# Weights of an output projection split during the attention heads, in buffers shared with a gated unit

## The chip, the cores and the metric

The kernel runs on one core of a Trainium2 chip. The metric is the device time of one launch in microseconds (us), lower is better. The kernel before takes 1459.13 us, the median of three runs (1458.34 to 1462.85).

TensorE multiplies matrices into PSUM banks (in the profile PE, and PEld for its weight loads), VectorE is DVE, ScalarE is ACT, GpSimd is POOL, and SyncE (SP) issues nearly all transfers. Each engine works through its own instructions in the order in which the program's scheduler has put them.

## The reference

One layer of a decoder, for 1024 prompt tokens and 8 x 4 sample tokens, all in float32:

```python
z  = h @ w_in                                # q, k, v, forget logits, SSM input u
a  = attention(q, k, v, log f)               # 8 heads x 64, causal, decay bias
s  = S5(u);  s = gelu(s);  s = s * sigmoid(s @ w_glu + b_glu)
h1 = LN1(alpha * h + concat(a, s) @ w_out)   # w_out: 1024 x 1024
e  = sigmoid(h1 @ w_pg + b_pg) * (p @ w_pe)
h2 = LN2(alpha * h1 + relu(h1 @ w_up)**2 @ w_down + e)
```

The sample tokens attend to a paged cache of 512 rows each (`cache_k`, `cache_v`).

## The kernel before, in words

Products are exact to nearly float32: each operand is split into a rounded high part and the remainder (`split`, line 156: a cast on ScalarE, then a subtraction, mostly on VectorE), and three matmuls are summed.

The stages follow each other: the input norm and the value projection, the SSM with the other projections (to 300 us), the heads (313 to 521 us), the output projection with LN1 (to 650 us), the embedding gate, and the feed-forward block (from 740 us).

**The gated unit** (`glu`, line 1069) runs in the background of the first heads, with tiles of its own pool `glu`: four `yf`, two `sg`, one `mo` (lines 1055 to 1060). `fill` (line 921) takes a step of a background generator wherever it is called: first all of `glu`, then `sample` (line 931), the attention of the sample tokens. That one loads 64 cache pages (`pg`, 256 KB each) through six buffers and works on through the tail of the last head.

**A head** has two halves. `weights(h)` (line 859) makes the scores of one block of 128 queries: two matmuls to a bank, a minimum on VectorE with the mask `msk`, the exponential on ScalarE into `row`. `values(h)` (line 887) goes through 12 blocks: transposes of `row`, a copy `pe` on ScalarE, a cast `ph` on VectorE, the remainder `pl` on POOL, two matmuls with the values into `po`. At the end of each half of the tokens the result `oh` goes to DRAM (line 916). The scores run one head ahead of the values. The operands of a head (`qa`, `qb`, `ka`, `kb`) come in eight loads (`loads`, line 840) into a pool `attq`, two buffers each, two heads ahead.

**The tail of the last head** starts when its scores are done. The pool `attq` closes (line 1151). In its room and behind it come `h1p`, for the normed stream (line 1152), and `woa`, for the split blocks 4 to 7 of `w_out` (line 1154), which belong to the SSM half of the projection. `load_wo` (line 1157) loads a block of 512 KB into one of two shared buffers `raw` and splits it; lines 1164 to 1165 do so for blocks 4 to 7. `half(i, 4)` (line 1176) then loads the SSM half of token tile i (`mx`, in the same `raw` buffers, line 1171), splits it, and multiplies it by these blocks; this is interleaved with the last eight steps of head 7's values (line 1229). The reciprocals of the softmax sums (`rl`, transposed into `rlt`) go out to DRAM and come back as `rb`. Then the attention pool closes (line 1233), blocks 0 to 3 are loaded and split in its room (line 1236), and the loop at line 1282 does the rest of the projection, tile by tile.

**What sets the order.** The program is traced in the order of the code; a scheduler then orders each engine's instructions by its own simulated times, earlier-traced ones first among those that are ready. So a load may be issued long before its place in the code: in the trace of before, two of the `w_out` blocks are loaded at 282.7 and 320.4 us, but split at 493 us. `tc.issue_after(x)` keeps what is traced under it behind the instruction x, and `newest` (line 165) is the last one traced on an engine.

Of the kernel before, what the change touches and what calls it, by code (L numbers as in the profile page):

```python
# [8 lines left out]
F32 = mybir.dt.float32  # L9
# [9 lines left out]
D = 1024  # L19
# [50 lines left out]
def fox_s5_step(tc, a, o):  # L70
# [85 lines left out]
    def split(x, hi, lo, e=V):  # L156
        S.copy(hi, x)  # L157
        tt(e, lo, x, f(hi), SUB)
# [665 lines left out]

    psum("psB", s=3, t=2, o=1, f=2)
    ptag[0] = "f"
    qctx, actx, h1bctx, h1ctx, smctx, gctx = (ExitStack() for _ in range(6))
    h1x = pool("h1x", stack=h1ctx, side="right")
    aq_ = pool("attq", 2, stack=qctx, side="right")
    gp = pool("glu", stack=gctx, side="right")  # L830

    def slot(j, d=F32R):
        return (h1x, h1b)[j // 2].tile([128, 2 * L * CB], d, tag=f"u{j}", name="u", bufs=1)

    msk = aq_.tile([128, 512], F32, name="msk", bufs=1)
    G.memset(msk[:, 0:384], 0.0)
    G.tensor_copy(msk[:, 384:512], cst[:, TRI:TRI + 128])
    ins_, vs_, rows = {}, {}, {}

    def loads(h):  # L840
        hs_ = slice(h * 64, h * 64 + 64)
        qa = aq_.tile([128, T], F32R, tag="qa", name="qa")
        qb = aq_.tile([68, T], F32R, tag="qb", name="qb")
        ka = aq_.tile([128, T], F32R, tag="ka", name="ka")
        kb = aq_.tile([68, T], F32R, tag="kb", name="kb")
        for j in range(2):
            SY.dma_start(out=f(qa[j * 64:j * 64 + 64]), in_=qd[0, hs_, 0:T])
            SY.dma_start(out=f(ka[j * 64:j * 64 + 64]), in_=kkd[j, hs_, 0:T])
        SY.dma_start(out=f(qb[0:64]), in_=qd[1, hs_, 0:T])
        SY.dma_start(out=f(kb[0:64]), in_=kkd[0, hs_, 0:T])  # L850
        SY.dma_start(out=f(qb[64:68]), in_=cad[h, 0:4])
        SY.dma_start(out=f(kb[64:68]), in_=cad[h, 4:8])
        ins_[h] = qa, qb, ka, kb
# [33 lines left out]
    def values(h):  # L887
        hs_ = slice(h * 64, h * 64 + 64)
        vr = vs_.pop(h)
        vv = ap_.tile([128, 8, 2, HD], F32R, tag="vv", name="vv")  # L890
        V.tensor_copy(vv[:, :, 0], vr)
        tt(G, vv[:, :, 1], vr, f(vv[:, :, 0]), SUB)
        for u in range(2):
            po = bank("po", "o")
            for j in range(4 * u + 4):
                i0 = max(j, 4 * u)
                n = 512 * (u + 1) - 128 * i0
                t = bank("tw", "t")[:, 0:n]
                for i in range(i0, 4 * u + 4):
                    PE.transpose(t[:, (i - i0) * 128:(i - i0) * 128 + 128], rows[h, i][:, j * 128:j * 128 + 128], ident)  # L900
                ph = ap_.tile([128, 512], F32R, tag="ph", name="ph", bufs=3)[:, 0:n]
                pl = ap_.tile([128, 512], F32R, tag="pl", name="pl", bufs=3)[:, 0:n]
                pe = ap_.tile([128, 512], F32, tag="pe", name="pe", bufs=4)[:, 0:n]
                S.copy(pe, t)
                V.tensor_copy(ph, pe)  # L905
                tt(G, pl, pe, f(ph), SUB)
                o = po[:, 512 - n:512]
                v = vv[:, j].rearrange("p a d -> p (a d)")
                PE.matmul(o, lhsT=v, rhs=ph, start=(j == 0), stop=False, skip_group_check=True)
                PE.matmul(o, lhsT=v, rhs=pl, start=False, stop=(j == 4 * u + 3), skip_group_check=True)  # L910
                yield
            ol = ap_.tile([64, 512], F32, tag="ol", name="ol", bufs=1)
            S.copy(ol, po[64:128])
            oh = ap_.tile([64, 512], F32, tag="oh", name="oh", bufs=2)
            tt(V, oh, po[0:64], ol, ADD)
            SY.dma_start(out=mixd[hs_, u * 512:u * 512 + 512], in_=oh)

# [134 lines left out]
    NB = L * CB  # L1052
    ys = []

    for n in range(2):
        gp.tile([128, NB], F32, tag="sg", name="sg", bufs=2)
    gp.tile([128, NT], F32, tag="mo", name="mo")

    def load_y(m):
        t = gp.tile([128, NB], F32, tag="yf", name="yf", bufs=4)  # L1060
        if m < 3:
            SY.dma_start(out=t, in_=yd[m])
        else:
# [5 lines left out]
    def glu():  # L1069
# [15 lines left out]
            yield 0.0  # L1085
        for m in range(4):
            hi, lo = (x[:, :, m % 2 * 128:m % 2 * 128 + 128] for x in w[m // 2])
            sg = gp.tile([128, NB], F32, tag="sg", name="sg", bufs=2)
            yf = ys[m]
            cuts = ((0, 364), (364, 364), (728, 360))  # L1090
            pgs = [bank("mmg", t) for t in "ffo"] if m == 0 else [None] * 3
# [11 lines left out]
                S.activation(out=sg[:, c0:c0 + n], in_=ps[:, :n], func=AF.Tanh, scale=0.5, bias=bglu[:, m:m + 1])  # L1103
                yield 1.85 if m else 0.0
            ts(V, sg, sg, 0.5, MUL, 0.5, ADD)
            mo = gp.tile([128, NT], F32, tag="mo", name="mo")
            yv = yf.rearrange("p (l c) -> p c l", l=L)
            sv = sg.rearrange("p (l c) -> p c l", l=L)
            tt(V, mo[:, 0:T].rearrange("p (c l) -> p c l", l=L), yv[:, 0:NC], sv[:, 0:NC], MUL)
            tt(V, mo[:, T:NT].rearrange("p (b t) -> p b t", t=4), yv[:, NC:CB, 4:8], sv[:, NC:CB, 4:8], MUL)  # L1110
            SY.dma_start(out=mixd[AW + 128 * m:AW + 128 * m + 128], in_=mo)
        gctx.close()

    ahead = (x for h in range(H) for x in weights(h))

# [8 lines left out]
    h1b = pool("h1b", stack=h1bctx)  # L1124
    bp = pool("smp", 2, stack=smctx)
    ap_ = pool("att", 2, stack=actx)
    bg += [glu(), sample(bp)]
    lsum = ap_.tile([128, H, 12], F32, name="lsum", bufs=1)
    fill(1e-3)
    vload(0)  # L1130
    for i in range(4):
        steps(1)
        fill(5)
        if i == 1:
            loads(1)
    for h in range(H - 1):
        for j, _ in enumerate(values(h)):
            if j < 4 or j % 2:
                steps(1)
# [8 lines left out]
        steps(1)  # L1148
        fill(.3)
    steps(1)  # L1150
    qctx.close()
    h1p = pool("h1", stack=h1ctx, side="right")
    woctx = ExitStack()
    woa = pool("woa", stack=woctx, side="right")
    wo = {}

    def load_wo(k, p, q, e=V):
        hi, lo = (p.tile([128, D], F32R, name=f"wo{n}{k}") for n in "hl")
        raw = q.tile([128, D], F32, tag="raw" if q is wp else "z", name="rawo", bufs=2 if q is wp else 3)
        SY.dma_start(out=raw, in_=a["w_out"][0][k * 128:(k + 1) * 128])  # L1160
        split(raw, hi, lo, e)
        wo[k] = hi, lo

    for k in range(4, 8):
        load_wo(k, woa, wp, V)
    mixv = mixd.rearrange("(k p) t -> p k t", p=128)
    dv = "p (c n) -> p c n"
    mxs, pss, order = {}, {}, [0, 1, 2, 3, 4, 5, 8, 6, 7]

    def load_mx(i):  # L1170
        mx = wp.tile([128, KD, 128], F32, tag="raw", name="mx", bufs=2)
        t0, r = tiles[i]
        SY.dma_start(out=mx[:, 4:8, :r], in_=mixv[:, 4:8, t0:t0 + r])
        return mx, [wp.tile([128, KD, 128], F32R, tag=t, name=t, bufs=2) for t in ("whi", "wlo")]

    def half(i, k0):
        t0, r = tiles[i]
        if k0:
            mxs[i] = load_mx(i)
            pss[i] = [bank("pso", t) for t in ("ss", "so")[order.index(i) % 2]]  # L1180
        mx, (mh_, ml_) = mxs[i]
        ks_ = slice(k0, k0 + 4)
# [32 lines left out]
            rb = rbs.pop(i)  # L1215
            tt(V, mx[:, 0:4, :r], mx[:, 0:4, :r], rb[:, :, :r], MUL)

    rl = ap_.tile([128, H, 8], F32, name="rl", bufs=1)
    tt(V, lsum[:, :, 4:8], lsum[:, :, 4:8], lsum[:, :, 8:12], ADD)
    V.reciprocal(rl, lsum[:, :, 0:8])  # L1220
    t = bank("trl", "t")[0:64, 0:128]
    PE.transpose(t, rl.rearrange("p h i -> p (h i)"), ident)
    rlt = ap_.tile([64, 128], F32, name="rlt", bufs=1)
    S.copy(rlt, t)
    SY.dma_start(out=rld.rearrange("h (i c) -> (h i) c", c=128), in_=rlt)
    for i in range(2):
# [7 lines left out]
    op = pool("out", 2, stack=smctx)  # L1234
    wop = pool("wob", stack=woctx, side="right")
    for k in range(4):
        load_wo(k, wop, op, V)
        next(ssm, None)
        fill(.5)
    for _ in ssm:  # L1240
# [2 lines left out]
        load_at(i)  # L1243


    ub = {(kh, 0): [h1p.tile([128, 4, HN], F32R, name=f"u{n}{kh}") for n in "hl"] for kh in range(2)}
    pend = []

    def gate(w, th, tag):
# [518 lines left out]
```

## Time and profile before

| | us |
|---|---|
| median of three runs | 1459.13 |
| the profiled execution | 1462.21 |
| its span, first to last instruction | 1460.4 |
| TensorE busy | 1383.8 |
| VectorE busy | 977.6 |
| POOL busy | 675.6 |
| ScalarE busy | 634.9 |
| mean granted clock of TensorE | 0.977 of 2.4 GHz |

The table shows one profiled execution; its time stands 3.1 us above the median. Busy times are unions of an engine's instructions. A row of the windows view gives a stretch, its length, the busy time and number of instructions of PE, PEld, DVE, ACT and POOL in it, TensorE's granted clock (1.00 is 2.4 GHz, 0.50 is 1.2 GHz), the share of the 16 DMA engines' time that was used, and GB/s. A timeline row gives an instruction's start and duration, and in brackets how long its engine was idle before it and what ended that.

### The profile page before, as it was taken

The page shows a single profiled execution, that of the slowest core. Times are in us where ns is not written, and L with a number is a line of the kernel's source. Part 1 is how long each engine was busy: PE and PEld are TensorE (multiplying, and loading weights), DVE is VectorE, ACT ScalarE, POOL GpSimd, SP SyncE. Part 2 cuts the span into 40 slices and gives each one's busy share as a digit, 9 for nine tenths or more (in the row PEclk, how much of TensorE's full clock was granted, in tenths as well). Part 3 has the DMA queues.
Part 4 walks back from the last instruction along what each step waited for, and adds up shares of the span by engine and source line. Part 5 has one row for each costly group of instructions (what it writes and reads, how often), then busy time and mean ns, then how long its engine had stood idle before and what let it go on. Part 6 is the DMA issues. An engine that isn't in the chain of part 4 may idle for free. (4 is left out here: it accounts for less than half of the span.)

```text
span 1460.4 us, 26638 instructions
## 1 busy us (share of the span) xinstructions
PE 1383.8 (95%) x10045; PEld 1268.7 (87%) x10045; DVE 977.6 (67%) x1579; ACT 634.9 (43%) x1188; POOL 675.6 (46%) x639
## 2 busy tenths in 40 slices
PE   6997999979999889999999999999999999999796
PEld 4887898967766656789999999999999999999786
DVE  7559599648877735657846555545455888788567
ACT  4333434445775623543325444444456443434212
POOL 4313012025665500018846433443347787777845
PEclk7999999989999989999999999999999999999998
DMA  7574355596776564313233444344457345546922
GB/s 275 177 136 105 89 153 144 159 233 177 182 175 173 150 205 118 102 42 114 69 103 125 162 162 140 120 146 163 148 196 273 121 136 163 162 161 172 181 66 101
DMA packets 209192, 218.38 MB, mean 150 GB/s; under 512 B 43976, under 2 KB 166472, under 8 KB 209064
## 3 DMA queue, kind: packets, MB, share of 16 engines
q1 hardware_dynamic: 197288, 178.02, 42.2%
q0 software_dynamic: 11776, 38.67, 8.3%
q8 instruction: 79, 1.29, 0.4%
q14 instruction: 49, 0.40, 0.1%
HBM read 143.59 MB, written 66.55 MB: 144 GB/s over the span
## 5 line engine op out<-in xcount | busy, mean ns | idle before, releaser
L1408 PE MATMUL pd<-x,a 128*128 128x264 f32 x1344 | 172.2, 287 | 10.2 <-POOL a L82 4.0
L1408 PEld LDWEIGHTS pd<-x,a 128*128 128x128 f32 x1344 | 167.8, 190 | 11.9 <-POOL a L82 5.1
L82 DVE TENSOR_TENSOR pacc<-pd,pacc 128x528 f32<-128x528 f32 x180 | 122.0, 700 | 64.5 <-PE pd L1408 63.6
L157 ACT CAST a<-s 128x256 fp32r<-128x256 f32 (+1 forms) x176 | 82.0, 483 | 183.6 <-PE pd L1408 75.6
L82 DVE TENSOR_TENSOR wlo<-raw,whi 128x1024 fp32r<-128x1024 f32 x68 | 104.4, 1535 | 43.7 <-ACT whi L157 32.7
L1408 PE MATMUL pb<-th,a 128*128 128x264 f32 x768 | 132.3, 284 | 0.0
L82 POOL TENSOR_TENSOR pl<-pe,ph 128x512 fp32r<-128x512 f32 (+1 forms) x96 | 100.4, 1054 | 67.6 <-DVE ph L905 44.9
L82 POOL TENSOR_TENSOR a<-s,a 128x256 fp32r<-128x256 f32 x112 | 104.9, 994 | 54.9 <-ACT a L157 54.6
L82 POOL TENSOR_TENSOR s<-raw 128x256 f32<-128x256 f32 (+1 forms) x72 | 79.5, 1155 | 84.9 <-DVE a L82 65.9
L1408 PEld LDWEIGHTS pb<-th,a 128*128 128x128 f32 x768 | 109.3, 189 | 0.0
L1408 PE MATMUL pd<-x,whi 128*128 128x264 f32 x672 | 109.1, 285 | 0.0
L82 DVE TENSOR_TENSOR x<-x 128x1056 fp32r<-128x1056 f32 (+2 forms) x68 | 95.6, 1437 | 8.4 <-ACT x L1429 7.4
L82 POOL TENSOR_TENSOR rs<-rs,mh 128x1 f32<-128x1 f32 (+1 forms) x27 | 20.5, 768 | 161.4 <-DVE rs L86 159.1
L183 PE MATMUL mmc<-hhi,whi 128*128 128x352 f32 x288 | 94.5, 328 | 0.0
L183 PE MATMUL mmc<-hhi,wlo 128*128 128x352 f32 x288 | 94.1, 327 | 0.0
L1408 PEld LDWEIGHTS pd<-x,whi 128*128 128x128 f32 x672 | 93.5, 188 | 0.2 <-DVE pacc L82 0.2
L183 PE MATMUL mmc<-hlo,whi 128*128 128x352 f32 x288 | 93.5, 325 | 0.0
L82 DVE TENSOR_TENSOR a<-s,a 128x512 fp32r<-128x512 f32 x64 | 47.4, 745 | 47.0 <-ACT a L157 42.7
L1408 PE MATMUL pb<-tl,a 128*128 128x264 f32 x384 | 78.1, 285 | 0.0
L157 ACT CAST whi<-raw 128x1024 fp32r<-128x1024 f32 x48 | 50.5, 1051 | 58.7 <-PE pa L1408 27.1
L882 ACT ACTIVATE row<-ss,nm 128x384 f32<-128x384 f32 (+4 forms) x96 | 55.5, 583 | 37.9 <-DVE nm L878 36.3
L1408 PE MATMUL pd<-x,wlo 128*128 128x264 f32 x336 | 68.3, 285 | 0.0
(470 smaller groups left out, 3961.9 us busy)
## 6 DMA issues: line engine op xcount, KB each, us to landing
x<-gd SPq DMA_DIRECT2D x53, 528.0 KB
raw<-in_w_up_dram SPq DMA_DIRECT2D x32, 512.0 KB
raw<-in_w_down_dram SPq DMA_DIRECT2D x120, 128.0 KB
gd<-e POOLq DMA_DIRECT2D x14, 1056.0 KB, 7.4
gd<-c POOLq DMA_DIRECT2D x14, 792.0 KB, 5.3
pg<-in_cache_k_dram SPq DMA_DIRECT2D x32, 256.0 KB
pg<-in_cache_v_dram SPq DMA_DIRECT2D x32, 256.0 KB
pacc<-pacc POOLq DMA_DIRECT2D x24, 264.0 KB, 7.0
```

Of the source, the lines that this page charges most:

```text
L82: e.tensor_tensor(out, x, y, op=op)
L157: S.copy(hi, x)
L183: PE.matmul(out, lhsT=wt[:, k], rhs=xt[:, k, c0:c0 + n], start=(k == 0 and i == 0), stop=(k == nk - 1 and i == 2))
L882: S.activation(out=pr_[:, c * n:(c + 1) * n], in_=ps, func=AF.Exp, scale=-1.0, bias=nm[:, i:i + 1], accum_out=lsum[:, h, i + 4 * c:i + 4 * ...
L1408: PE.matmul(ps[:, p, :PC], lhsT=wt[:, k], rhs=xt[:, k, p * PC:(p + 1) * PC], start=(start and k == 0 and j == 0), stop=(k == n - 1 and j = ...
```

## The change

The pool `glu` gets eight buffers `g0` to `g7` that stay until the projection's end. The gated unit's tiles use `g0` to `g6`, and the split blocks 4 to 7 of `w_out` take the same buffers two by two. `load_wo` for these blocks moves from the tail of the last head to the starts of heads 2 to 5, one block to a head, and its load is kept behind SP's newest instruction. At the start of head 6 the SSM halves of token tiles 0 and 1 are loaded. The operands of a head share four buffers with the normed stream: `qa` and `qb` are two parts of one tile, `ka` and `kb` of another. `oh` has one buffer, `rl` and `rlt` use `pe`'s buffers, and the mask moves to the attention pool, so it is made after the normed input stream is freed.

```diff
-    aq_ = pool("attq", 2, stack=qctx, side="right")
-    gp = pool("glu", stack=gctx, side="right")
+    h1p = pool("h1", stack=h1ctx, side="right")
+    gp = pool("glu", stack=woctx, side="right")
+    def hslot(j):
+        return h1p.tile([128, 4 * HN], F32R, tag=f"h{j}", name=f"h{j}")
+    def gslot(j, shape, d=F32):
+        return gp.tile(shape, d, tag=f"g{j}", name=f"g{j}")
+    for j in range(8):
+        gslot(j, [128, L * CB if j < 6 else NT if j == 6 else D])
...
     def loads(h):
-        qa = aq_.tile([128, T], F32R, tag="qa", name="qa")
-        qb = aq_.tile([68, T], F32R, tag="qb", name="qb")
-        ka = aq_.tile([128, T], F32R, tag="ka", name="ka")
-        kb = aq_.tile([68, T], F32R, tag="kb", name="kb")
+        qt, kt = (hslot(h % 2 * 2 + j) for j in range(2))
+        qa, qb, ka, kb = qt[:, 0:T], qt[0:68, T:2 * T], kt[:, 0:T], kt[0:68, T:2 * T]
...
-            oh = ap_.tile([64, 512], F32, tag="oh", name="oh", bufs=2)
+            oh = ap_.tile([64, 512], F32, tag="oh", name="oh", bufs=1)
...
-        t = gp.tile([128, NB], F32, tag="yf", name="yf", bufs=4)
+        t = gslot(m, [128, NB])
...
-            sg = gp.tile([128, NB], F32, tag="sg", name="sg", bufs=2)
+            sg = gslot(4 + m % 2, [128, NB])
...
-            mo = gp.tile([128, NT], F32, tag="mo", name="mo")
+            mo = gslot(6, [128, NT])
...
+    msk = ap_.tile([128, 512], F32, name="msk", bufs=1)
+    G.memset(msk[:, 0:384], 0.0)
+    G.tensor_copy(msk[:, 384:512], cst[:, TRI:TRI + 128])
...
+    def load_wo(k, q, e=V):
+        if k > 3:
+            hi, lo = (gslot(2 * k - 8 + j, [128, D], F32R) for j in range(2))
+        else:
+            hi, lo = (wop.tile([128, D], F32R, name=f"wo{n}{k}") for n in "hl")
+        raw = q.tile([128, D], F32, tag="raw" if q is wp else "z", name="rawo", bufs=2 if q is wp else 3)
+        with ExitStack() as st1:
+            if k > 3:
+                st1.enter_context(tc.issue_after(newest(mybir.EngineType.SP)))
+            SY.dma_start(out=raw, in_=a["w_out"][0][k * 128:(k + 1) * 128])
+        split(raw, hi, lo, e)
...
     for h in range(H - 1):
+        if 2 <= h < 6:
+            load_wo(h + 2, wp, V)
+        elif h == 6:
+            mxs.update((i, load_mx(i)) for i in range(2))
...
-    for k in range(4, 8):
-        load_wo(k, woa, wp, V)
...
         if k0:
-            mxs[i] = load_mx(i)
+            if i not in mxs:
+                mxs[i] = load_mx(i)
...
-    rl = ap_.tile([128, H, 8], F32, name="rl", bufs=1)
+    rl = ap_.tile([128, 512], F32, tag="pe", name="rl", bufs=4)[:, 0:8 * H].rearrange("p (h i) -> p h i", h=H)
...
-    rlt = ap_.tile([64, 128], F32, name="rlt", bufs=1)
+    rlt = ap_.tile([128, 512], F32, tag="pe", name="rlt", bufs=4)[0:64, 0:128]
...
-    ub = {(kh, 0): [h1p.tile([128, 4, HN], F32R, name=f"u{n}{kh}") for n in "hl"] for kh in range(2)}
+    ub = {(kh, 0): [hslot(2 * kh + j).rearrange("p (k n) -> p k n", k=4) for j in range(2)] for kh in range(2)}
```

## Rows read from the trace of the kernel before

**Rows 1.** The page, part 1: busy us of TensorE, its share of the span, instructions.

```profile
PE 1383.8 (95%) x10045; PEld 1268.7 (87%) x10045; DVE 977.6 (67%) x1579; ACT 634.9 (43%) x1188; POOL 675.6 (46%) x639
```

**Rows 2.** The windows view, heads 2 to 5.

```profile
384.00:404.00 20.00, 19.78 (x149) 15.67 (x147) 17.89 (x41) 15.08 (x42) 14.40 (x15) 1.00 0.73 181
404.00:424.00 20.00, 18.84 (x154) 14.72 (x152) 15.53 (x42) 14.44 (x42) 12.27 (x13) 1.00 0.65 149
424.00:451.00 27.00, 26.42 (x125) 14.56 (x126) 15.02 (x37) 13.97 (x38) 15.14 (x15) 0.94 0.77 207
451.00:471.00 20.00, 20.00 (x148) 15.89 (x147) 15.88 (x37) 15.08 (x43) 11.89 (x12) 1.00 0.65 164
```

**Rows 3.** The same view, head 7's tail and after it.

```profile
490.00:512.00 22.00, 17.50 (x170) 12.75 (x170) 16.48 (x26) 13.18 (x26) 12.49 (x11) 0.97 0.70 196
508.00:512.00 4.00, 1.09 (x4) 0.71 (x3) 0.83 (x2) 0.78 (x2) 1.18 (x2) 0.81 1.08 300
512.00:517.00 5.00, 5.00 (x13) 3.95 (x13) 4.86 (x14) 2.68 (x5) 0.46 (x1) 0.50 0.45 120
...
540.00:545.00 5.00, 3.84 (x6) 0.65 (x7) 1.23 (x1) 1.04 (x1) 0.00 (x0) 0.66 0.56 156
```

**Rows 4.** Timeline, first pause: start, us, engine, line, operation, count [idle before <- releaser].

```profile
502.85 0.58 SPq L1173 DMA_DIRECT2D mx<-mixd  x1
...
505.82 0.33 PE L900 MATMUL tw<-cst,row 128*128 128x128 f32 x1
...
510.52 0.62 ACT L1183 CAST whi<-mx 128x512 fp32r<-128x512 f32 x1 [6.22 <-DMA mx<-mixd]
...
511.04 0.26 ACT L904 COPY pe<-tw 128x128 f32<-128x128 f32 x1
...
511.19 0.80 PE L1196 MATMUL pso<-woh,whi 128*128 128x512 f32 x1 [2.91 <-ACT whi L1183]
...
515.30 0.63 PE L1196 MATMUL pso<-woh,wlo 128*128 128x512 f32 x1
...
518.07 0.40 PE L1196 MATMUL pso<-wol,whi 128*128 128x512 f32 x1
```

**Rows 5.** Instructions on the tile rawo: ns min/median/max, first and last start.

```profile
L157 ACT CAST woh<-rawo x8: 1044/1048/1072, 493.1 to 542.1; 128x1024 fp32r<-128x1024 f32 x8
L82 DVE TENSOR_TENSOR wol<-rawo,woh x8: 1210/1226/1846, 494.2 to 543.2; 128x1024 fp32r<-128x1024 f32 x8
```

**Rows 6.** Timeline, VectorE and POOL in head 7's tail.

```profile
504.79 1.21 DVE L82 TENSOR_TENSOR wol<-rawo,woh 128x1024 fp32r<-128x1024 f32 x1
...
503.30 1.28 POOL L82 TENSOR_TENSOR pl<-pe,ph 128x512 fp32r<-128x512 f32 x1 [1.56 <-DVE ph L905]
...
505.01 2.12 POOL L82 TENSOR_TENSOR pl<-pe,ph 128x512 fp32r<-128x512 f32 x1 [0.43 <-DVE ph L905]
```

**Rows 7.** Timeline, second pause: loads of rawo, their casts, TensorE's wait.

```profile
521.62 1.50 SPq L1160 DMA_DIRECT2D rawo<-in_w_out_dram  x3
...
525.40 1.05 ACT L157 CAST woh<-rawo 128x1024 fp32r<-128x1024 f32 x1 [0.97 <-DMA rawo<-in_w_out_dram]
...
528.03 0.39 SPq L1160 DMA_DIRECT2D rawo<-in_w_out_dram  x1
...
540.85 1.62 PE L1035 MATMUL po<-pg,u 128*32 128x512 f32 x2 [3.85 <-DMA pg<-in_cache_v_dram]
...
542.12 1.04 ACT L157 CAST woh<-rawo 128x1024 fp32r<-128x1024 f32 x1 [13.16 <-DMA rawo<-in_w_out_dram]
```

**Rows 8.** Timeline of SP, two transfers of oh.

```profile
404.44 0.54 SPq L916 DMA_DIRECT2D mixd<-oh  x1
...
410.08 0.47 SPq L916 DMA_DIRECT2D mixd<-oh  x1
```

**Rows 9.** Timeline, TensorE's first score.

```profile
313.44 0.45 PE L872 MATMUL ss<-kb,qb 68*128 68x128 f32 x1 [5.83 <-DMA kb<-kkd]
```

More of the change, by code (lines that the diff above doesn't have):

```diff
@@ L826, in fox_s5_step @@
     ptag[0] = "f"
-    qctx, actx, h1bctx, h1ctx, smctx, gctx = (ExitStack() for _ in range(6))
+    actx, h1bctx, h1ctx, smctx, woctx = (ExitStack() for _ in range(5))
     h1x = pool("h1x", stack=h1ctx, side="right")
-    aq_ = pool("attq", 2, stack=qctx, side="right")
-    gp = pool("glu", stack=gctx, side="right")
+    h1p = pool("h1", stack=h1ctx, side="right")
[6 more added lines that the diff above has]
+        gslot(j, [128, L * CB if j < 6 else NT if j == 6 else D])
     def slot(j, d=F32R):
         return (h1x, h1b)[j // 2].tile([128, 2 * L * CB], d, tag=f"u{j}", name="u", bufs=1)
-    msk = aq_.tile([128, 512], F32, name="msk", bufs=1)
-    G.memset(msk[:, 0:384], 0.0)
-    G.tensor_copy(msk[:, 384:512], cst[:, TRI:TRI + 128])
     ins_, vs_, rows = {}, {}, {}
@@ L1053, in fox_s5_step @@
     ys = []
-    for n in range(2):
-        gp.tile([128, NB], F32, tag="sg", name="sg", bufs=2)
-    gp.tile([128, NT], F32, tag="mo", name="mo")
     def load_y(m):
-        t = gp.tile([128, NB], F32, tag="yf", name="yf", bufs=4)
+        t = gslot(m, [128, NB])
         if m < 3:
@@ L1135, in fox_s5_step, with load_mx @@
             loads(1)
+    wo = {}
+    def load_wo(k, q, e=V):
[9 more added lines that the diff above has]
+        split(raw, hi, lo, e)
+        wo[k] = hi, lo
+    mixv = mixd.rearrange("(k p) t -> p k t", p=128)
+    mxs, pss, order = {}, {}, [0, 1, 2, 3, 4, 5, 8, 6, 7]
+    def load_mx(i):
+        mx = wp.tile([128, KD, 128], F32, tag="raw", name="mx", bufs=2)
+        t0, r = tiles[i]
+        SY.dma_start(out=mx[:, 4:8, :r], in_=mixv[:, 4:8, t0:t0 + r])
+        return mx, [wp.tile([128, KD, 128], F32R, tag=t, name=t, bufs=2) for t in ("whi", "wlo")]
     for h in range(H - 1):
+        if 2 <= h < 6:
+            load_wo(h + 2, wp, V)
+        elif h == 6:
+            mxs.update((i, load_mx(i)) for i in range(2))
         for j, _ in enumerate(values(h)):
@@ L1150, in fox_s5_step @@
     steps(1)
[L1151 to L1162, printed above, removed]
-    for k in range(4, 8):
-        load_wo(k, woa, wp, V)
-    mixv = mixd.rearrange("(k p) t -> p k t", p=128)
-    dv = "p (c n) -> p c n"
[L1168 to L1174, printed above, removed]
+    dv = "p (c n) -> p c n"
     def half(i, k0):
```

3 lines of the change are left out of this document (1 added, 2 removed).

## The prediction

> **What bounds the kernel now.** I read the windows view first, to see which engine is never idle. Over the whole span TensorE is busy for 1383.8 of 1460.4 us [rows 1], so the end is set by TensorE's own work, by its idle time and by the stretches at the lower of its clocks. An edit that moves work of other engines gains only what it takes from those two, so the place to look is where TensorE idles near the code that is changed.
>
> Heads 2 to 5, where the change puts work, are nearly full: four stretches, 384 to 471 us, in which TensorE is idle for 0.22, 1.16, 0.58 and 0.00 us, 1.96 us in 87 [rows 2]. The tail of head 7, from which work is taken, is not: from 490 to 512 us TensorE is busy for 17.50 of 22 us, so 4.50 us are idle [rows 3]. The timeline says why [rows 4]. The SSM half of the first token tile (`mx`) is issued by SP at 502.85. Its cast on ScalarE starts at 510.52, after 6.22 us in which ScalarE waited for that load. The last copy `pe` of head 7's probabilities stood behind it: its transpose was over at 506.15 (505.82 + 0.33), but the copy ran at 511.04. TensorE waited 2.91 us and went on at 511.19 with the first matmul of the output projection. In that pause the granted clock fell: 0.81 in the row 508 to 512, 0.50 (1.2 GHz) from 512 to 517 [rows 3]. The same matmul that takes 0.40 us at 518.07 takes 0.63 us at 515.30 [rows 4].
>
> **What it removes.** (1) The wait for `mx`. The loads of tiles 0 and 1 move from behind the last scores to the start of head 6, at about 471, some 30 us earlier, so their 7.7 us (502.85 to 510.52) lie beside TensorE's work. They can start there, since the raw buffers are free once the weights of heads 4 and 5 are split. I count the 2.91 us whole. (2) The low clock behind it. Of the 5.00 us from 512 to 517, 2.5 are lost if all work halves its pace, 1.8 by the two durations (5.00 x (1 - 0.40/0.63)). Before 512, 1.5 us of low clock (4 x 0.19 / 0.5) cover the last 0.8 us of work and cost 0.4. That is 2.2 to 2.9; I take 2.5. (3) The splits of the four blocks `wo4` to `wo7` leave the tail: four casts of 1.05 us on ScalarE and four subtractions of 1.23 us (up to 1.85) on VectorE [rows 5], 9.1 us of two engines that also make head 7's `pe` and `ph`. The rest of the idle time there is 4.50 - 2.91 = 1.59 us, of many causes; between nothing and all of it I take half, 0.8. Removed: 2.9 + 2.5 + 0.8 = 6.2 us.
>
> **What it adds.** (4) The same four casts and subtractions come in heads 2 to 5, one pair to a head. If they are covered, they cost nothing; if the cover is gone, all 9.1 us. VectorE is busy for 17.89 of 20 us in head 2, so 1.23 to 1.85 us more nearly fill it. In heads 3, 4 and 5 it has 4.5, 12.0 and 4.1 us left, ScalarE 5 to 13 [rows 2]. I take 1.0 us for head 2 and 0.2 for each of the others, 1.6, near the low end, because the other three rows show room. Late next, where a pair does not fit, is `ph` on VectorE, then POOL's `pl`, then the value matmul.
>
> The pair also meets POOL. The subtraction that starts at 504.79 lies beside a `pl` of 2.12 us, while the `pl` of the same shape at 503.30 took 1.28 [rows 6]: 0.84 us more. The Trainium skill (SBUF — State Buffer, section Who interferes with whom) says that a VectorE instruction with two inputs in SBUF and a GpSimd instruction that reads SBUF cannot run together, and that the later one waits for the whole of the other. By that rule the four subtractions would take 3.4 us from POOL wherever they lie, and the sum would fall by as much if POOL sets the pace; the two rows agree with its direction. I do not count this, since POOL is busy for 14.40, 12.27, 15.14 and 11.89 us in these heads [rows 2], but it is a rival below.
>
> (5) Four loads of 512 KB are issued in heads 2 to 5, with an order that keeps each behind SP's newest instruction. Each takes 0.4 us of SP's queue (the row at 528.03 [rows 7]), ahead of pages and head loads, and 2.9 us of transfer at the 181 GB/s of head 2. At a DMA share of 0.65 to 0.77 there, 5.4 to 7 us in each head are spare [rows 2], so I count nothing for the transfers; without that cover a page or a head's operands come up to 2.9 us later, and TensorE's transposes of the page wait. ScalarE's cast now waits for such a load, and everything behind it on ScalarE with it (`pe`, the exponentials); that is the rival of the other side. (6) `oh` has one buffer instead of two, so its write waits until the earlier transfer has landed. Two such transfers are issued 5.6 us apart, at 404.44 and 410.08 [rows 8]. Landings of larger loads take 3.8 us (521.62 to 525.40) to 14.1 us (528.03 to 542.12) [rows 7]. The transfer is a quarter of their size, so I take the short one and count 0; with the long one VectorE would be held for some 9 us (14.1 less the 5.0 us between the issue and the next write), once. (7) `rl` and `rlt` use two of the four `pe` buffers, for the few us of the reciprocal's way out. That holds a copy at most until that transfer has landed, 3.8 us by the same row, and I count 0, since the other two buffers serve meanwhile. (8) The mask is made after the normed stream is freed, by two POOL instructions of 384 and 128 columns, together less than the 1.28 us of a 512-wide `pl`. The first score waits for its operand `kb` until 313.44 and has idled 5.83 us by then [rows 9], which hides it; without that cover it costs those 1.28 us at most. (9) One tile for each head's `qa` and `qb`, and one for `ka` and `kb`: the same eight loads in the same order, double-buffered as before: 0.
>
> **The sum.** 6.2 - 1.6 = 4.6 us. The profiled execution took 1462.21 us (span 1460.4), which is 3.1 over the median of the runs. So 1457.6 against its own time, and 1459.1 - 4.6 = **1454.5 us** against the median. A measurement of this kernel can tell about 0.3% from no change, 4.4 us: the borders are 1454.7 and 1463.5.
>
> **The rivals.** *More is won.* A second pause follows: TensorE waits 3.85 us, until 540.85, for pages of `cache_v`, and the clock falls again (0.66 from 540 to 545, that is 3.4 us at half pace, which can cost 1.7) [rows 3, 7]. The pages compete with the loads of `wo0` to `wo3`. These start when head 7 ends, and head 7 ends earlier by more than TensorE's work does, if its `pe` no longer stands behind `mx`. Of the 5.6 us I let 4.5 come on top: 1450. Against it: the same bytes still have to come in the same stretch.
>
> *What is won is lost again.* If that second pause is set by transfers whose start does not move, the 6.2 us come back as a longer wait for pages, and 1.6 remains at most: 1459 to 1460.7. It includes the case that the scheduler, which reorders by its own estimates, puts little elsewhere. For it speaks that SP sends the pages behind the loads; against it that those loads start at head 7's end, which moves forward.
>
> *Slower: ScalarE held by a raw block.* The place is the cast of `wo4` to `wo7` in heads 2 to 5, behind the eight loads of a head. The scheduler put the cast of `mx` so early that ScalarE stood 6.22 us, and TensorE paid 2.91 idle and 2.5 at the low clock, 5.4. A block's load takes 3.8 to 14.1 us, so the same can happen up to four times. One such event: -4.6 + 5.4, about no change. Two decide: -4.6 + 10.8 = +6.2, 1465. Against it: the first cast after head 7 waited 0.97 us [rows 7], not 6, and the pairs can slide.
>
> *POOL held by the subtractions.* 3.4 us more, as worked out above: 1454.5 + 3.4 = 1457.9, no measurable change.
>
> The Trainium skill (DMA: Bandwidth & Descriptors, section Anatomy of one DMA) gives for one transfer about 2.0 us and the bytes over 436 GB/s, an estimate of 3.2 us for a block, for another kind of queue than SP's. By it ScalarE would not be held at all; the rows, 3.8 to 14.1, are above it, and they decide.
>
> **The numbers.** Forecast 1454.5 (own range 1451 to 1457.5): 0.42, of which 0.24 lie under the border of 1454.7. More won: 0.20. Lost again: 0.18. Slower: 0.14. POOL held: 0.06. Faster by over 0.3% is 0.24 + 0.20 = 0.44; slower 0.14; within it the rest, 0.42. The range leaves out the lower end of the second case and the upper half of the slower one: 1447.5 to 1464.
>
> **What would show it.** Right: the casts of `wo4` to `wo7` in heads 2 to 5, one each; `mx` of tiles 0 and 1 issued near head 6; no ScalarE wait for `mx` before the projection's first matmul; granted clock 1.0 through head 7's tail; TensorE idle under 2 us there, and under 4 us in heads 2 to 5. Wrong: ScalarE waits for `rawo` of over 3 us inside a head, a low clock in heads 2 to 5, VectorE waits at `oh` for a transfer, or a wait for pages of over 4 us behind head 7.

## The result: slower, outside the range

The changed kernel took 1469.02 us in the median (5 runs, 1468.21 to 1473.91), the kernel before 1461.28 beside it: a ratio of 1.0064 [1.0046, 1.0082]. Run again with 12 runs it took 1467.14, ratio 1.0045 [1.0029, 1.0062]. The forecast was 1454.5, the range 1447.5 to 1464.

The profiled execution took 1468.21 us (span 1466.4). The page, part 1, of the changed kernel:

```profile
PE 1389.0 (95%) x10045; PEld 1273.2 (87%) x10045; DVE 979.1 (67%) x1579; ACT 634.6 (43%) x1188; POOL 674.5 (46%) x639
```

Every engine has the same number of instructions as in [rows 1], so work was only moved. The windows view of the changed kernel, with the stretches of [rows 2, 3]: length, TensorE busy, weight loads, VectorE, ScalarE, POOL, granted clock, DMA share, GB/s:

```profile
384.00:404.00 20.00, 19.26 (x167) 15.64 (x166) 17.77 (x39) 15.59 (x42) 13.16 (x13) 1.00 0.79 209
404.00:424.00 20.00, 18.93 (x158) 15.05 (x158) 17.21 (x43) 13.85 (x40) 12.21 (x13) 1.00 0.76 178
424.00:451.00 27.00, 23.64 (x107) 13.50 (x108) 16.28 (x38) 15.81 (x42) 13.06 (x13) 0.94 0.80 216
451.00:471.00 20.00, 18.25 (x106) 11.26 (x104) 13.41 (x30) 11.29 (x29) 8.97 (x9) 1.00 0.87 210
490.00:512.00 22.00, 22.00 (x138) 17.56 (x137) 11.72 (x29) 11.87 (x33) 9.43 (x10) 1.00 0.22 63
512.00:517.00 5.00, 4.81 (x38) 3.42 (x36) 2.29 (x3) 2.35 (x5) 2.83 (x3) 1.00 0.27 57
526.00:536.00 10.00, 7.05 (x19) 5.23 (x19) 4.68 (x12) 2.69 (x5) 0.77 (x1) 0.66 0.85 273
540.00:545.00 5.00, 5.00 (x23) 4.04 (x22) 1.14 (x2) 0.00 (x0) 0.00 (x0) 1.00 0.74 208
```

The wait for `mx` is gone: the two loads are issued at 463.5 and 469.0 us and cast at 470.6 and 473.5. From 490 to 512 us TensorE is never idle (22.00 of 22, where it was 17.50), and the clock is 1.00 there and in the stretches where it fell to 0.50 and 0.66 [rows 3]. But these rows compare times, not the same work: the last score stands at 490.2 us before and at 500.5 in the changed kernel, 10 us later. Its tail has a pause of its own further on: TensorE waits for head 7's last output, and the granted clock is 0.66 from 526 to 536 us, where it was 1.00 before.

```profile
529.36 1.22 PE L1204 MATMUL pso<-g,whi 128*128 128x512 f32 x2 [1.99 <-DVE oh L82]
```

And heads 2 to 5, with 1.96 us idle before, now have 0.74 + 1.07 + 3.36 + 1.75 = 6.92. The timeline of the changed kernel (start, us, engine, line, operation, count, idle before and its releaser) shows the four casts and one of their subtractions:

```profile
393.19 1.05 ACT L157 CAST g<-rawo 128x1024 fp32r<-128x1024 f32 x1 [1.73 <-DMA rawo<-in_w_out_dram]
413.46 1.05 ACT L157 CAST g<-rawo 128x1024 fp32r<-128x1024 f32 x1 [0.49 <-DMA rawo<-in_w_out_dram]
414.54 1.90 DVE L82 TENSOR_TENSOR g<-rawo,g 128x1024 fp32r<-128x1024 f32 x1
436.12 1.05 ACT L157 CAST g<-rawo 128x1024 fp32r<-128x1024 f32 x1 [0.65 <-DMA rawo<-in_w_out_dram]
466.08 1.05 ACT L157 CAST g<-rawo 128x1024 fp32r<-128x1024 f32 x1 [1.87 <-DMA rawo<-in_w_out_dram]
```

And TensorE's waits in the same timeline, one in head 2 and those from 424 to 471 us, where before there was a single one, of 0.67 us:

```profile
394.77 0.55 PE L904 MATMUL tw<-cst,row 128*128 128x128 f32 x3 [0.61 <-ACT pe L908]
...
425.96 0.55 PE L904 MATMUL tw<-cst,row 128*128 128x128 f32 x3 [0.65 <-ACT pe L908]
426.86 0.55 PE L904 MATMUL tw<-cst,row 128*128 128x128 f32 x3 [0.35 <-ACT pe L908]
429.10 0.66 PE L1024 MATMUL tpp<-cst,u 128*128 128x128 f32 x4 [1.69 <-DVE u L86]
438.44 1.04 PE L904 MATMUL tw<-cst,row 128*128 128x128 f32 x7 [0.67 <-ACT pe L908]
...
468.40 1.04 PE L904 MATMUL tw<-cst,row 128*128 128x128 f32 x7 [1.30 <-ACT pe L908]
```

Three stand right behind a cast (0.61, 0.67 and 1.30): the copy `pe` that frees a transpose's bank was queued behind it on ScalarE. The others come at other places of the order: TensorE waits for `pe`, or for the sample's probabilities from VectorE. The largest of them, 2.69 us together from 425 to 429, stand where the softmax of the sample meets the head's copies, 7 us ahead of the next cast; before, such waits took 1.74 us, from 422 to 425.

### The profile page after: what moved, and what is told of

The parts are those of the page before. It is cut to its first block, busy times and chain, and to the rows that moved or that the text cites. A ratio compares the mean times of both kernels' runs of the same rounds, so it can differ in the third digit from the quotient of the medians.

```text
span 1466.4 us, 26629 instructions
## 1 busy us (share of the span) xinstructions
PE 1389.0 (95%) x10045; PEld 1273.2 (87%) x10045; DVE 979.1 (67%) x1579; ACT 634.6 (43%) x1188; POOL 674.5 (46%) x639
## 5 line engine op out<-in xcount | busy, mean ns | idle before, releaser
L1416 PE MATMUL pa<-h,whi 128*128 128x264 f32 x512 | 85.9, 285 | 1.4 <-ACT c L1493 0.7
```

The lines of the kernel that those rows point to most:

```text
L1416: PE.matmul(ps[:, p, :PC], lhsT=wt[:, k], rhs=xt[:, k, p * PC:(p + 1) * PC], start=(start and k == 0 and j == 0), stop=(k == n - 1 and j = ...
```

## The experiments

As a common measure I use two stretches of the windows view, TensorE's idle time in 384 to 490 us (heads 2 to 6) and idle time plus low clock (length times one less the granted clock) in 490 to 580 us (the tail). Their two rows, of before and then of the changed kernel:

```profile
384.00:490.00 106.00, 104.05 (x708) 75.60 (x706) 78.99 (x188) 71.51 (x199) 64.55 (x63) 0.98 0.64 163
490.00:580.00 90.00, 81.35 (x430) 56.85 (x430) 46.78 (x83) 34.09 (x63) 15.04 (x15) 0.94 0.60 175
```

```profile
384.00:490.00 106.00, 98.37 (x685) 69.61 (x684) 81.97 (x182) 70.71 (x189) 60.09 (x58) 0.98 0.73 187
490.00:580.00 90.00, 83.28 (x463) 59.49 (x462) 46.45 (x91) 34.48 (x76) 19.67 (x21) 0.96 0.54 164
```

So heads: 1.95 before, 7.63 after; tail: 8.65 + 5.4 = 14.1 before, 6.72 + 3.6 = 10.3 after. The low clock inside the heads is not in the measure, nor what lies before 384 or behind 580 us. The same for every run, each from its one profiled execution:

| run | splits of weights 4 to 7 | heads, idle | tail, idle + clock | median, us | ratio to before |
|---|---|---|---|---|---|
| before | after the last scores | 2.0 | 14.1 | 1461 | 1 |
| after, e8 | heads 2 to 5 | 7.6, 8.3 | 10.3, 8.8 | 1469.0, 1467.1 | 1.0064, 1.0045 |
| e6 | heads 2 to 5 | 8.6 | 10.4 | 1468.9 | 1.0048 |
| e3 | heads 2 to 5, loads a head ahead | 7.2 | 13.8 | 1476.3 | 1.0089 |
| e4, e13 | heads 2 to 5, two `oh` | 7.0, 7.2 | 10.2, 9.6 | 1465.4, 1468.3 | 1.0032, 1.0056 |
| e11 | heads 2 to 5, on POOL | 8.2 | 15.0 | 1473.8 | 1.0083 |
| e12 | heads 2 to 5, twice | 9.8 | 12.6 | 1472.0 | 1.0071 |
| e1 | slipped to 320 to 360 us | 2.5 | 19.5 | 1474.7 | 1.0079 |
| e2 | slipped to 319 to 360 us | 3.1 | 14.0 | 1465.1 | 1.0024 |
| e5 | after the last scores | 2.6 | 11.8 | 1460.8 | 0.9992 |
| e9 | after the last scores | 2.1 | 16.9 | 1463.8 | 1.0010 |
| e10 | after the last scores | 3.0 | 18.5 | 1464.9 | 1.0025 |
| e14 | after the last scores | 2.5 | 10.5 | 1458.9 | 0.9986 |
| e15 | after the last scores | 2.1 | 15.7 | 1469.8 | 1.0065 |
| e16 | after the last scores | 2.7 | 8.1 | 1459.1 | 0.9988 |
| e17 | after the last scores | 3.3 | 4.0 | 1461.6 | 1.0010 |
| e18 | after the last scores | 3.3 | 16.0 | 1460.4 | 0.9994 |
| e19 | after the last scores | 2.2 | 19.9 | 1465.8 | 1.0030 |

Three of these times hold more than the table shows. From the last projection matmul to the end, in code that their edits don't touch, e1, e3 and e15 take 829.4, 830.9 and 830.8 us, where the kernel before takes 824.9 and the changed one 824.7. No run shows why.

### Splits in other places

**e1, all back in the tail by program order.** The two lines that keep a load behind SP's newest instruction go as well.

```diff
-        if 2 <= h < 6:
-            load_wo(h + 2, wp, V)
-        elif h == 6:
-            mxs.update((i, load_mx(i)) for i in range(2))
...
+    for k in range(4, 8):
+        load_wo(k, wp, V)
```

> All of the new buffers stay (shared gated-unit buffers, head operands in the normed stream's slots, one oh, rl and rlt in pe's buffers, the mask in the attention pool), but blocks 4 to 7 are loaded and split in the tail of head 7 again, and the SSM halves of tiles 0 and 1 are loaded there too. Theory A (the splits in heads 2 to 5 cost what was lost): the result of head 7's first half is written at 498 to 501 us instead of 511, and the time is that of the kernel before within 0.3%: 1457 to 1465. Theory B (the new buffers cost it: the single oh, the shared pe, the mask, or the pause at 353 us): the heads stay late by 8 us or more although no split lies in them, and since the tail's gain is gone too, the time is 1470 to 1477.

1474.71 us, ratio 1.0079 [1.0058, 1.0101]. It doesn't test what it was to test: without the order on SP the scheduler moved the loads to 283 to 353 us, as soon as the gated unit had left the slots, and the splits with them into heads 0 and 1. (In the kernel before, the weights lay over the operands of the last heads, which held them back by themselves.) It shows that nothing is won in heads 0 and 1 either: TensorE idles for 7.5 us from 313 to 384 us, where it was 3.8 before.

**e2, without that order alone.**

```diff
-            if k > 3:
-                st1.enter_context(tc.issue_after(newest(mybir.EngineType.SP)))
```

> The changed kernel without the order that keeps each of the four loads of w_out behind SP's newest instruction. Theory A1 (ScalarE and all behind it stand because the block is loaded too late, 4.7 us of waits for rawo in heads 2 to 5): if the scheduler now issues some of the loads a head earlier, those waits fall to under 2 us, TensorE's idle time from 384 to 490 us falls from 7.6 us by 3 or more, and the time by 3 to 6 us, to 1463 to 1466. Theory A2 (the cast and the subtraction themselves break up the heads' rhythm): the waits may fall, but the heads stay late, 1467 to 1471. Theory B: no change, 1467 to 1471.

1465.11 us, 1.0024 [1.0013, 1.0035]: the same slip, with 5.9 us idle from 313 to 384 us, so the same reservation.

**e5, truly behind the heads.** The buffers of the change stay. The splits are held behind the last exponential and the last minimum of head 7.

```diff
+    with tc.issue_after(last[0]), tc.issue_after(last[1]):
+        for k in range(4, 8):
+            load_wo(k, wp, V)
```

> The changed kernel with all its new buffers (shared slots, operand tiles, one oh, mask in the attention's pool), but the loads and splits of weights 4 to 7 are put back behind the heads: each cast is held on ScalarE behind the last exponential of head 7 and each subtraction on VectorE behind the last minimum of head 7, and the mixed tiles are loaded behind them, as before. Theory S (the splits placed in heads 2 to 5 cost the heads their time): the heads run as before, the tail has its old waits, so 1461 us, 1459 to 1463. Theory B (the shared buffers cost it, the single oh above all): heads late as in the changed kernel and the tail as before, so 1468 us or more.

1460.78 us, ratio 0.9992 [0.9978, 1.0007]: the kernel before, within the measurement. Shared slots, operand tiles, the single `oh`, the mask and `rl` in the attention's pool cost nothing that can be seen, together. Two of the four blocks are still loaded in the heads, at 437.2 and 437.7 us, and the heads are not late, so a load there does not make them late by itself. The loss is in where the splits (and the mixed tiles) stand; e10 and e14 below, with the mixed tiles early and the splits late, leave the splits.

**e12, the splits twice.** The same cast and subtraction are done again, to the same result.

```diff
-        split(raw, hi, lo, e)
+        for _ in range(2 if k > 3 else 1):
+            split(raw, hi, lo, e)
```

> The changed kernel with each of the four splits in heads 2 to 5 done twice over (the same cast and the same subtraction again). Theory S: twice the work in the heads costs once more what it cost, less what the tail gains: the changed kernel lost 5 to 8 us by the median, its tail won some 3, so the heads lost 8 to 11 and the time comes to 1474 us, 1470 to 1480. If the work itself is covered and only the change of order counts: 1466 to 1470 us.

1471.96 us, 1.0071 [1.0052, 1.0089]; TensorE's idle time in the heads is 9.8 us, against 7.6 and 8.3 with the splits once and 2.0 without. In idle time the second one adds 1.6 to 2.2 us where the first added 5.7 to 6.3; in the times the intervals of e12 and of the changed kernel overlap, so there a dose is not shown. It would fit that part of the loss is the work, and part the order that the first split disturbs; this run does not tell them apart.

### What in the splits it is

**e3, loads one head ahead.** `load_raw` is the part of `load_wo` that issues the load.

```diff
         if 2 <= h < 6:
-            load_wo(h + 2, wp, V)
+            load_wo(h + 2, wp, V, raws.pop(h + 2))
...
+        if 1 <= h < 5:
+            raws[h + 3] = load_raw(h + 3, wp)
```

> Each block of w_out is loaded one head ahead of its split (blocks 4 to 7 loaded at the starts of heads 1 to 4, split at the starts of heads 2 to 5), still behind SP's newest instruction. Theory A1 (late loads): no wait of ScalarE for rawo is left in the heads, the lag of head 6's second half against the kernel before falls from 10 us to 3 to 6, and the time to 1461 to 1465. Theory A2 (the splits themselves): the waits are gone but the lag stays at 8 us or more and the time at 1467 to 1471. Theory B: 1467 to 1471.

1476.33 us, 1.0089 [1.0061, 1.0117]. Of its four casts only the first still waits for its block, 0.80 us at 374 us, and TensorE idles for 7.2 us in the heads all the same. That the transfer comes late is not the cause. The time lies above every range that was expected; 6 us of it arise behind the projection, as said above.

**e11, on POOL.**

```diff
-        split(raw, hi, lo, e)
+        if k > 3:
+            G.tensor_copy(hi, raw)
+            tt(G, lo, raw, f(hi), SUB)
+        else:
+            split(raw, hi, lo, e)
```

> The changed kernel with the casts and the subtractions of the four weights in heads 2 to 5 moved from ScalarE and VectorE to GpSimd. If the hold of ScalarE by the cast (1.05 us and its wait for the transfer) is what makes PE wait in the heads: 1463 to 1465 us. If any of the three engines that feed PE costs the same when it is held, GpSimd with two steps of some 2 us each costs as much or more: 1467 to 1472 us, with PE waiting for pl.

1473.79 us, 1.0083 [1.0065, 1.0100], worse than on the other two. Instructions on the tile `rawo` in this run (ns min/median/max, first and last start):

```profile
L1151 POOL CAST g<-rawo x4: 1037/1038/1042, 391.9 to 474.9; 128x1024 fp32r<-128x1024 f32 x4
L82 POOL TENSOR_TENSOR g<-rawo,g x4: 2360/2370/2507, 396.9 to 481.0; 128x1024 fp32r<-128x1024 f32 x4
```

A pair holds POOL for 3.4 us, and the idle time in the heads is 8.2 us, as with the splits on the other two engines. But the waits are others than was expected: none of TensorE's in 384 to 490 us ended with POOL's `pl`; 3.40 us in one piece were for pages of `cache_v` (at 433.79), the rest for VectorE and the scores' exponentials. So taking the pair off ScalarE and VectorE saves nothing; why the heads are late here is not shown.

**e4 and e13, two `oh`.** `ol` and `oh` become one tile with two buffers.

```diff
-            ol = ap_.tile([64, 512], F32, tag="ol", name="ol", bufs=1)
-            S.copy(ol, po[64:128])
-            oh = ap_.tile([64, 512], F32, tag="oh", name="oh", bufs=1)
-            tt(V, oh, po[0:64], ol, ADD)
+            oh = ap_.tile([64, 512], F32, tag="oh", name="oh", bufs=2)
+            S.copy(oh, po[64:128])
+            tt(V, oh, po[0:64], oh, ADD)
```

> The changed kernel with two buffers for oh again: the copy of the lower half on ScalarE and the sum on VectorE go to the same tile, of which there are two, so the room is the same. Theory A: one wait of VectorE for the transfer of oh (1.9 us) goes, and the time falls by 0 to 2 us, 1467 to 1469. Theory B, in the form that the single oh holds VectorE in the heads: the time falls by 4 us or more, to 1465 or less.

> The changed kernel with the two halves of a head's output in one tile with two buffers, a second time, beside the other runs of this set: 1465.4 us as the first time if the one oh costs 2 to 3 us in the changed kernel (PE's wait of 2.0 us for it in the tail), 1467 to 1469 if the first time was chance.

1465.37 us the first time, 1468.34 the second (1.0032 and 1.0056, intervals 1.0015 to 1.0049 and 1.0038 to 1.0074). The first looked like a gain; the second does not bear it out. The one `oh` has no cost that can be told here.

**e8, unedited.**

> The changed kernel once more, unedited, so that the other runs of this set stand beside it: 1469 us, 1467.5 to 1470.5. A median under 1466.5 would mean that the excess of the changed kernel is in part the phase of its clock and not its order.

1467.14 us over 12 runs, from 1464.17 to 1472.66, at granted clocks of 0.970 to 0.979; it is just below the expected range and not under 1466.5. The profiled one was the fastest of them.

### Why the tail pays so little back

**e6, without the early mixed tiles.**

```diff
-        elif h == 6:
-            mxs.update((i, load_mx(i)) for i in range(2))
```

> The changed kernel, with only the early load of the first two mixed tiles (and so their early casts) taken out: the splits stay in heads 2 to 5. Theory S: the heads are as late as in the changed kernel and the tail waits for the mixed tile again, some 3 us, and perhaps the low clock behind it: 1471 to 1475 us. Theory M (the work of the mixed tiles inside head 7 is what makes the heads late): 1466 us or less.

1468.92 us, 1.0048 [1.0031, 1.0064], within the intervals what e8 and the changed kernel took, and between the two theories; the tail loses 10.4 us, where theirs loses 8.8 and 10.3. But it is no test of the early load, since the scheduler put the loads at the same place without being told:

```profile
463.57 0.39 SPq L1159 DMA_DIRECT2D mx<-mixd  x1
```

The second follows at 470.22; in the changed kernel they stand at 463.51 and 469.03.

**e9 and e10, splits behind head 7, loads at head 6.** The raw blocks go into the operand tiles that head 6 has left; the splits are held as in e5. In e10 the mixed tiles' loads are held at head 6 as well, and `oh` has two buffers.

```diff
+        if h == 6:
+            mxs.update((i, load_mx(i)) for i in range(2))
...
+                for j in range(2):
+                    rw = h1p.tile([128, 4 * HN], F32, tag=f"h{j}", name="rw")
+                    for k in range(2):
+                        raws[4 + 2 * j + k] = rw[:, k * D:(k + 1) * D]
+                        SY.dma_start(out=raws[4 + 2 * j + k], in_=a["w_out"][0][(4 + 2 * j + k) * 128:(5 + 2 * j + k) * 128])
```

> The changed kernel, but the four raw blocks of the weights are loaded at head 6 into the operand tiles of head 6 after its scores (they are free there), the splits are held behind the last exponential and the last minimum of head 7, and the first two mixed tiles are loaded at head 6 as in the changed kernel. No split stands in heads 2 to 5 and no transfer is late in the tail. Theory S: the heads as before, and the tail without the wait for the mixed tile (2.9 us) and most of the low clock behind it (2.5 us): 1456 us, 1453 to 1459. Theory B: heads late as in the changed kernel, 1463 us or more.

> Splits held behind the last exponential of head 7, their raw blocks loaded at head 6 into the operand tiles that head 6 has left, and, other than in the run with the same loads before, the mixed tiles' loads kept in their place at head 6 in SyncE's order, and the two halves of a head's output in one tile with two buffers. Theory S (splits in heads 2 to 5 are the loss): heads as before until 490 us within 1 us, and the tail without the wait for the mixed tile and for the one oh: 1457 us, 1454 to 1460. Rival L (the gain of the tail is lost again, since PE then waits for the pages of the sample and runs at the low clock there): 1460 to 1463 us.

1463.75 us, 1.0010 [0.9994, 1.0026], and 1464.85, 1.0025 [1.0012, 1.0038]. In e9 the mixed tiles' loads slipped to 355 us and the order of the sample with them. In e10 nothing slipped: from 384 to 471 us its heads write their results within 0.6 us of the kernel before. And yet the tail loses 18.5 us, more than before, and the time lies above both ranges. Its windows rows:

```profile
490.00:512.00 22.00, 19.67 (x131) 15.05 (x129) 11.30 (x21) 10.85 (x22) 7.60 (x7) 1.00 0.38 110
512.00:545.00 33.00, 25.09 (x151) 16.99 (x151) 14.77 (x24) 8.65 (x16) 5.11 (x5) 0.89 0.69 208
```

and TensorE's waits in the tail of e10, in the timeline:

```profile
513.66 0.75 PE L906 MATMUL tw<-cst,row 128*128 128x128 f32 x3 [3.23 <-ACT pe L910]
...
524.64 1.22 PE L1213 MATMUL pso<-g,whi 128*128 128x512 f32 x2 [1.69 <-DVE oh L82]
...
542.55 1.05 PE L1040 MATMUL po<-pg,u 128*32 128x512 f32 x2 [1.93 <-DMA pg<-in_cache_v_dram]
...
546.11 1.91 PE L1040 MATMUL po<-pg,u 128*32 128x512 f32 x2 [2.51 <-DMA pg<-in_cache_v_dram]
```

The first projection matmul stands at 496.5 us, 14.7 earlier than before. The reading that e14 is to test: it is filler; done early, it takes TensorE from the sample's last key step (515.9 instead of 501.9) and from head 7 (its last output at 523.9 instead of 520.3), and it is missing later, when `pe`, head 7's last output and the value pages are waited for.

**e14, the filler held back.** As e10, with these matmuls behind the sample's last key step (`keys[1]`). The sample's steps are also taken faster until then (`fill(2.5)` instead of `fill(.3)`).

```diff
-        if j % 2:
-            next(ssm, None)
-        fill(.3)
+        if j % 2 and 1 in keys:
+            with tc.issue_after(keys[1]):
+                next(ssm, None)
+        fill(2.5 if 1 not in keys else .3)
```

> The run with loads at head 6 and splits behind head 7, with the state-space half of the first two tiles of the projection held behind the last key step of the sample, where it stood before the change. Theory P (the half that came early took PE from head 7 and from the sample, and the later steps wait for just these): the half no longer pushes them back, no wait for the mixed tile, 1458 us, 1455 to 1460.5. Rival T (the end of the tail is set by transfers that open only with the end of head 7, and PE's order before that is without effect): 1463 to 1466 us as in the run without the hold.

1458.94 us, ratio 0.9986 [0.9975, 0.9998]; the first projection matmul is at 512.2, head 7's last output at 521.7. That is 5.9 us less than e10, as the reading foretold, though the hold and the faster sample steps are not told apart. As far as the interval goes it is the only order, with e16, that is ahead of both kernels, by 1.7 us. Its profiled execution took 1464.82 us, the most of its twelve, so its trace shows less of the gain.

**e15 and e18, the mixed tiles loaded in the tail.** As e10 without the early load (e15); in e18 also

```diff
-            if i not in mxs:
-                mxs[i] = load_mx(i)
+            with tc.issue_after(newest(mybir.EngineType.SP)):
+                mxs[i] = load_mx(i)
```

> The same loads at head 6 and splits behind head 7, but the mixed tiles loaded in the tail as before the change, so the state-space half cannot start before some 511 us. Theory P: the last step of head 7 (oh 7.1) falls back to 520 to 521 us and the time to 1461 us, 1459 to 1462.5, though the wait for the mixed tile is back. Rival T: 1463 to 1466 us.

> The run with the late mixed tiles once more, now with their loads held in their place in SyncE's order in the tail (in the run before they had slipped ahead to 353 us, and the state-space half stood at 494 us as early as ever). Theory P (the early half takes PE from head 7 and the sample): the first projection matmul at 511 us or later, the last step of head 7 at 519 to 521 us, the heads as before, and 1460 us, 1458 to 1462. Rival T (the end of the tail is set by transfers that open with the end of head 7): no better than with the early half, 1463 to 1466 us.

In e15 the loads slipped to 353 us and the first projection matmul to 494.5, so it is no test; it took 1469.79 us, and 6 us of its excess arise after 1079 us, in code that no edit touches, part of it at a clock of 0.73 in 1380 to 1400 us, where it was 0.89 before. e18 took 1460.38, 0.9994 [0.9981, 1.0007], with the wait for the mixed tile back (2.02 us at 506.8, which is 4 us earlier than was expected).

**e16, e17 and e19, raw blocks of weights 0 to 3 loaded after the last scores** into head 7's operand tiles: on e15, on e14 and on e18.

```diff
+            rw = h1p.tile([128, 4 * HN], F32, tag=f"h{2 + j}", name="rv")
...
-        load_wo(k, op, V)
+        wo[k] = tuple(wop.tile([128, D], F32R, name=f"wo{n}{k}") for n in "hl")
+        split(raws[k], *wo[k], V)
```

> As the run with the late mixed tiles, and the raw blocks of weights 0 to 3 loaded, after the last scores, into the operand tiles of head 7, which are free then, and not behind the end of head 7. Rival T (these four transfers and the pages behind them on SyncE's queue set the pause at 540 us, where the kernel before lost 4.2 us idle and 4.3 us of low clock in 512 to 545): 1457 us, 1454 to 1459. Theory P alone (the pause comes from the sample's order): no gain, 1460 to 1462 us.

> Both: the state-space half held behind the sample's keys with its mixed tiles loaded early, and the raw blocks of weights 0 to 3 loaded after the last scores. If P and T each hold for their own pause, the two add: 1454 us, 1451 to 1457. If only one of them counts, the time of that one alone.

> The same, and the raw blocks of weights 0 to 3 loaded after the last scores into the operand tiles of head 7. Rival T: 4 to 6 us less than the run with the held loads alone, 1455 us, 1453 to 1458. Theory P alone: no less than that run by more than 1.5 us.

1459.10 us (0.9988 [0.9978, 0.9998]), 1461.59 (1.0010 [0.9997, 1.0022]) and 1465.76 (1.0030 [1.0016, 1.0043]). Against the run that each is built on, this is 10.7 less, 2.7 more and 5.4 more: the two gains do not add. Of the 10.7, the profiled executions show 4.9 up to the last projection matmul (636.0 and 631.1 us) and as much behind it, in code that no edit touches. In e19 part of the loss can be read in SP's queue and in TensorE's wait:

```profile
489.87 3.06 SPq L1194 DMA_DIRECT2D rv<-in_w_out_dram  x4
504.10 0.58 SPq L1160 DMA_DIRECT2D mx<-mixd  x1
```

```profile
511.62 2.07 PE L1218 MATMUL pso<-g,whi 128*128 128x512 f32 x4 [4.86 <-ACT whi L1205]
```

The mixed tile is issued behind the four blocks, 3.7 us later than in e18 (1.7 us of it e19 was late already, at 477.1 us), and the wait for it grew from 2.02 to 4.86 us. In the profiled executions of e17, e18 and e19 the account of idle time and clock does not close with the time at which the gate starts (by some 5 us), so I don't read their tails further.

## Why the prediction was wrong, step by step

**Step 4, the splits in heads 2 to 5, failed.** It was sized at 1.6 us, "because the other three rows show room". Measured: TensorE's idle time in heads 2 to 6 grows by 5.0 to 6.7 us in every run that has the splits there once (after, e8, e3, e4, e6, e13, and e11 on POOL), and by at most 1.4 us in every run with them after the last scores. The bounds, 0 to 9.1, held it; the choice near the low end was wrong. The error was to read room from busy shares. In 424 to 451 us VectorE was free for 12 us of 27 and ScalarE for 13 [rows 2], and just there TensorE lost the most (0.58 to 3.36). What counts is not whether the engine is free for 1.05 us somewhere in the head but what stands behind the cast when it runs: a `pe`, for which TensorE waits within 1 or 2 us. That is read in the trace for 2.6 us of the 7.6 (the three waits right behind casts). The rest lies elsewhere in the order; that it follows from the splits is shown by the runs without them, by which steps is not.

**Steps 1 and 2, the wait for `mx` and the low clock,** were right as far as the mechanism goes: the wait is gone. The low clock is gone from its place, but comes again 16 us later behind another wait (0.66 from 526 to 536 us), so "granted clock 1.0 through head 7's tail" did not hold. And 5.4 us was the wrong price. With the heads late no run shows what the early load is worth, since e6 has it too; with the heads on time and the filler held it is worth about 1.4 us by the medians (e14 against e18, whose intervals overlap). The time came back as other waits: in e10 all of it and 4 us more. That is the rival "what is won is lost again". Its cause was named as transfers whose start does not move; the runs speak rather for TensorE's order (e14), and moving those transfers helped in one order and hurt in two. What sets the tail in general stays open.

**Step 3** can't be told apart: moving the splits out of the tail is the same edit as step 4.

**Steps 5 to 9 at nothing** were right: e5 has all the buffers, and is at 0.9992. For step 5, e3 shows that the loads' time is not what counts. On step 6, e4 and e13 find no cost.

**The sum.** The profiled executions differ by 6.0 us in their spans, and three stretches account for that. From the first score (313.4 us before, 313.0 in the changed kernel) to the last (490.2 and 500.5) the changed kernel takes 10.7 us longer: TensorE is idle there for 12.4 us instead of 5.4, and the granted clock is 0.95 instead of 0.96. From there to the last projection matmul (635.5 and 641.7) it takes 4.1 us less, and what lies before and behind takes 0.6 less. So the forecast of 6.2 us less in the tail and 1.6 more in the heads went wrong most of all in the heads. Not all of the 10.7 is the splits: 0.9 us of the idle time arises before 384 us, ahead of the first cast. In the profiled execution of the changed kernel TensorE idled 2.40 us at 350 to 366 us and the clock there was 0.75; in e8, the same program, it did not idle there and the clock was 0.84. In e5 it idled 2.67 us there, and its median is that of the kernel before. e8's profiled execution has 9.5 us more in the heads, 6.6 less in the tail, and its span is 2.0 us longer than that of before; but it lies 3.0 us below its own median.

**The rivals.** "ScalarE held by a raw block", 1465, had the side and nearly the size, but not the cause. ScalarE's waits for `rawo` were 1.73, 0.49, 0.65 and 1.87 us, none near the 6 of the model, and e3 took them away without a gain. "More is won" did not come. "POOL held by the subtractions" did not either: the `pl` nearest to the subtractions kept their 1.27 to 1.30 us. Once the two met, and it was VectorE's instruction that was longer: 1.90 us at 414.54 while a `pl` ran from 414.08 to 415.36. The Trainium skill (SBUF — State Buffer, section Who interferes with whom) says that the later of the two waits for the other. That agrees nearly: 0.82 us were left of the `pl`, and the subtraction took 0.68 us more than its 1.22, once in four pairs.

## What to carry to other kernels

Work that is moved off a stall into a stretch where TensorE hardly idles need not be covered by the other engines' free share: look at what stands behind it on its engine, and how soon TensorE needs that. A pause that is closed with work that was to be done later anyway only moves, unless whatever ends the stretch (here the sample's keys, head 7's last output, the value pages) comes earlier too. In this kernel that rests on e10 and e14 alone. And when an edit takes away a buffer conflict, it may take away the only thing that held an instruction in its place: see in the trace where it went before reading a verdict from it.

## What was not expected

A second split in the same place cost about a third of the first in idle time (1.6 to 2.2 us against 5.7 to 6.3). The subtraction of 128x1024 took 2.37 us on POOL against 1.22 on VectorE, while the cast took 1.04 us on POOL and 1.05 on ScalarE. One kernel's executions spread over 8.5 us (e8, 1464.17 to 1472.66), so that a single profiled execution can show a third of the difference of the medians (2.0 of 5.4 us).
